# Two query groups whose weight tiles stream half of the tokens at a time: 256 + 128 columns in one, 128 columns throughout in the other

## The chip, the cores and the metric

The kernel runs on one NeuronCore of a Trainium2 chip. The metric is the device time of one execution in microseconds. The engines that matter here are TensorE (PE in the profile; its weight loads are listed apart as PEld), VectorE (DVE), ScalarE (ACT), and SyncE (SP), whose queue issues most transfers.

## The reference: what is computed

A decoder trunk of two layers over 256 tokens of width 2048, in float32: first a pooling mixer with a gated feed-forward part, then attention over one shared K and V with another gated feed-forward part. The change lies in the second layer, in one of three projections of the stream h (256 × 2048):

```python
k_shared = (h @ shared_w_k).reshape(B_, S, N_HEADS, HEAD_DIM)
v_shared = (h @ shared_w_v).reshape(B_, S, N_HEADS, HEAD_DIM)
...
q = (h @ w_q).reshape(B_, S, N_HEADS, HEAD_DIM)
```

Each weight matrix is 2048 × 2048, for 16 heads of 128. Behind them come three dilated causal windows, merged by their softmax denominators, and the output projection w_o.

## The kernel before

**Numbers.** A float32 product is made of three products of the format fp32r: each weight tile is split into a high part wh (ACT, line 82) and a low part wl (DVE, line 83), each activation likewise, and high × high, high × low and low × high are added up in PSUM. Low × low is left out.

**Units.** The whole program is a list of units. A unit is a weight tile of 512 rows by 512 columns (four blocks of 128 rows, k, by four blocks of 128 columns, m). `ahead` (line 110) issues the transfer of a unit's weights up to 5 units ahead on the SyncE queue, and the split up to 3 units ahead. `run_units` (line 125) takes one unit after the other: its matmuls, then whatever is due. `later(n, fn)` (line 119) puts work off by n units; what is due is counted in units.

**A unit's matmuls.** `mm_quad` (line 149) makes 16 pairs of (k, m). The activations of one quarter of the width lie in a tile `q` of shape 128 × 4 (k) × 2 (high, low) × 258, with 256 tokens used; they are the moving operand. A weight block of 128 × 128 is the stationary operand. In the mode "ab", which most units use, a pair is two matmuls: `h[:, k, c]` streams high and low side by side, 512 columns (line 164), into a PSUM bank of 512 columns, and `l[:, k, c]` streams the high part alone, 256 columns, onto the first half of that bank (line 165). The halves of the bank are added when it is read out. Modes "a" and "x" make three matmuls of 256 or 258 columns onto the first half (lines 167 to 169). Four banks, one for each m, collect four units (one group). In the last unit of a group the pairs go block by block (m outside, k inside), in the others k is outside. The first matmul onto a bank in a group clears it (`start`).

**The attention stage.** For hq = 0 to 3 (line 961) there are a k group, a q group and a v group of four units each. `group_tm` (the v groups) holds the activations stationary and streams weights, 512 columns each (lines 230 to 232). `qk_post` (line 856) reads a q or k group out of its banks: ACT copies the second half of a bank, DVE adds the first (lines 873, 874). Two and three units after a q group come its `scores` (line 883). `outputs` (line 948) of an hq runs four and seven units after its v group, so between the units of the next q group: matmuls at lines 956 and 957, then a split of the result on ACT and DVE (lines 958, 959) that gives the bank back. PSUM has 8 banks that all of these take in turn.

**Order.** Everything is emitted by hand in this order; each engine executes its own instructions in the order of emission and waits for others by semaphores.

Of the kernel before, what the change touches and what calls it, by code (L numbers as in the profile page):

```python
# [18 lines left out]
P = 128  # L19
# [13 lines left out]
def trunk(ctx: ExitStack, tc: tile.TileContext, x, pool_w_in, pool_w_grp, pool_scale, pool_w_out,  # L33
# [3 lines left out]
    V, A, PE = nc.vector, nc.scalar, nc.tensor  # L37
# [10 lines left out]
    def bank(nm):  # L48
        return psp.tile([P, 512], F32, name=nm, tag="ps")
# [69 lines left out]
    def later(n, fn):  # L119
        if n == 0:  # L120
            fn()
        else:
            pending.append([n, fn])
# [25 lines left out]
    def mm_quad(xq, ps, first, last, mode, mid, shifted):  # L149
        def go(h, l):  # L150
            nk, nb = h.shape[1], h.shape[2] // P
            order = [(k, m) for k in range(nk) for m in range(nb)]
            if last:
                order = [(k, m) for m in range(nb) for k in range(nk)]
            if first:
                for m in range(nb):
                    ps.append(bank("acc"))
            q = xq()
            n = XW if mode == "x" else T
            for i, (k, m) in enumerate(order):  # L160
                c = slice(m * P, (m + 1) * P)
                st, sp = first and k == 0, last and k == nk - 1
                if mode == "ab":
                    PE.matmul(ps[m], h[:, k, c], q[:, k, :, :T], start=st, stop=False)  # L164
                    PE.matmul(ps[m][:, :T], l[:, k, c], q[:, k, 0, :T], start=False, stop=sp and not shifted)  # L165
                else:
                    PE.matmul(ps[m][:, :n], h[:, k, c], q[:, k, 0, :n], start=st, stop=False)  # L167
                    PE.matmul(ps[m][:, :n], h[:, k, c], q[:, k, 1, :n], start=False, stop=False)  # L168
                    PE.matmul(ps[m][:, :n], l[:, k, c], q[:, k, 0, :n], start=False, stop=sp and not shifted)  # L169
                if sp and shifted:  # L170
                    PE.matmul(ps[m][:, :T], neg1, ST["cs"], start=False, stop=True)
                if mid is not None and i == 7:
                    mid()
        return go

    def group(w, r0s, c0, ncol, xqs, post, mode="ab", mids=(), shifted=False):
        ps = []
        for j, (r0, nr) in enumerate(r0s):
            last = j == len(r0s) - 1
            units.append((w[r0:r0 + nr, c0:c0 + ncol],  # L180
                          mm_quad(xqs[j], ps, j == 0, last, mode, mids[j] if j < len(mids) else None, shifted),
                          (lambda: post(ps)) if last else None))
# [98 lines left out]
    rows4 = [(512 * j, 512) for j in range(4)]  # L281
# [14 lines left out]
    xsrcs = [lambda j=j: XC[j] for j in range(4)]  # L296
# [146 lines left out]
    def norm_evac(ps, nb, tmp, dst):  # L443
        wgb = lnp.tile([P, 4, 2], F32, name="wgb", tag="wgb", bufs=2)
        for m in range(nb):
            A.copy(wgb[:, m, :], ps[m][:, T:XW])
        for m0 in range(0, nb, 2):
            ts = [(m, tmp()) for m in range(m0, min(nb, m0 + 2))]
            for m, t in ts:
                V.tensor_tensor(t, ps[m][:, :T], ST["rs"], OP.mult)  # L450
            for m, t in ts:
                V.scalar_tensor_tensor(t, ST["mr"], wgb[:, m, 0:1], t, op0=OP.mult, op1=OP.subtract)
                A.activation(dst(m), t, AF.Identity, scale=-1.0, bias=wgb[:, m, 1:2])
# [388 lines left out]
    def v_post(c):  # L842
        def post(t, ps):
            if t == 0:
                vts[c] = pools["attn"].tile([P, 2, 512], F32, name="vt", tag="vt")
                A.copy(vts[c][:, 0, :], ps)
            else:
                V.tensor_copy(vts[c][:, 1, :], ps)
                if c == 3:
                    later(1, lambda: transposes(c, (0, 1)))  # L850
                    later(2, lambda: transposes(c, (2, 3)))
                later(2 if c == 3 else 4, lambda: outputs(c, (0, 1)))
                later(3 if c == 3 else 7, lambda: outputs(c, (2, 3)))
        return post

    def qk_post(nm, hq):
        def post(ps):
            later(2 if hq == 0 and nm == "k" else 0, lambda: evac(ps))

        def evac(ps):  # L860
            ap = pools["attn"]
            o = ap.tile([P, 4, T], F32, name=nm, tag=nm)
            qk[nm] = o

            def tmp():
                return ap.tile([P, T], F32, name="qt", tag="t1", bufs=2)

            if hq == 0 and nm == "k":
                norm_evac(ps, 4, tmp, lambda m: o[:, m, :])
            else:  # L870
                for m in range(4):
                    t = tmp()
                    A.copy(t, ps[m][:, T:])
                    V.tensor_tensor(o[:, m, :], ps[m][:, :T], t, OP.add)
            if nm == "q":
                later(2, lambda: scores(hq, range(0, 2)))
                later(3, lambda: scores(hq, range(2, 4)))
                if hq < 3:
                    later(4, lambda: blocks(hq, (0, 1)))
                    later(7, lambda: blocks(hq, (2, 3)))  # L880
        return post

    def scores(hq, ms):
        ap = pools["attn"]
        for m in ms:
            ps = bank("s")
            q, k = qk["q"][:, m, :], qk["k"][:, m, :]
            PE.matmul(ps[:, 0:P], q[:, :P], k[:, :P], start=True, stop=True)
            PE.matmul(ps[:, P:3 * P], q[:, P:], k, start=True, stop=True)
            if m % 2 == 0:  # L890
                two = ap.tile([P, 2, 3, P], F32, name="p", tag="p", bufs=2)
            s = two[:, m % 2]
            sf, nf, cf = (t.rearrange("p a b -> p (a b)") for t in (s, negm, cnt))
            V.scalar_tensor_tensor(sf, ps[:, :3 * P], scale, nf, op0=OP.mult, op1=OP.add)
            mx = ap.tile([P, 6], F32, name="mx", tag="mx", bufs=4)
            parts = ((0, slice(0, P)), (1, slice(P, 3 * P)))
            for t, sl in parts:
                V.tensor_reduce(mx[:, t:t + 1], sf[:, sl], AX.X, OP.max)
            V.tensor_scalar(mx[:, 2:4], mx[:, 0:2], -1.0, None, op0=OP.mult)
            for t, sl in parts:  # L900
                A.activation(sf[:, sl], sf[:, sl], AF.Exp, bias=mx[:, 2 + t:3 + t])
            pr[hq, m] = (s, mx, two)
        for m in ms:
            s, mx, _ = pr[hq, m]
            sf, cf = (t.rearrange("p a b -> p (a b)") for t in (s, cnt))
            for t, sl in parts:
                V.scalar_tensor_tensor(sf[:, sl], sf[:, sl], 1.0, cf[:, sl], op0=OP.mult, op1=OP.mult,
                                       accum_out=mx[:, 4 + t:5 + t])
            V.reciprocal(mx[:, 0:2], mx[:, 4:6])
            for t, sl in parts:  # L910
                V.tensor_scalar(sf[:, sl], sf[:, sl], mx[:, t:t + 1], None, op0=OP.mult)
# [18 lines left out]
    def blocks(hq, ms):  # L930
        two = pr.pop((hq, ms[0]))[2]
        pr.pop((hq, ms[1]))
        b = hp.tile([P, 6 * P], F32, name="pb", tag="h")
        V.transpose(b, two.rearrange("p h s k -> p (h s k)"))

        t = turned(hq, ms)
        to = t.rearrange("p h s -> p (h s)").rearrange("p (k a j) -> p a k j", k=6, a=4)
        fr = b.rearrange("p (k b j) -> p b k j", k=6, b=4)

        def move(rows):  # L940
            for i in rows:
                for j in range(4):
                    nc.sync.dma_start(to[32 * j:32 * j + 32, i], fr[32 * i:32 * i + 32, j])

        later(1, lambda: move((0, 1)))
        later(2, lambda: move((2, 3)))
# [14 lines left out]
    for hq in range(4):  # L961
        x0 = hq == 0
        group(shared_w_k, rows4, 512 * hq, 512, psrcs if x0 else xsrcs, qk_post("k", hq), mode="x" if x0 else "ab")
        group(attn_w_q[0], rows4, 512 * hq, 512, xsrcs, qk_post("q", hq))
        group_tm(shared_w_v, rows4, 512 * hq, 512, xsrcs, v_post(hq))
    add_last(attn_w_o[0], rows4, [lambda j=j: oq[j] for j in range(4)], True, 1, 0, after=to_tokens)
    marks.append(len(units))
# [4 lines left out]
    with tc.tile_pool(name="start", bufs=1) as stp:  # L972
        for q in range(NQ):
            for t in range(2):
                XIN[q, t] = stp.tile([P, 512], F32, name=f"xin{q}{t}")
            halves = [slice(0, 256), slice(256, 512)] if q == 0 else [slice(0, 512)]
# [130 lines left out]
```

## Time and profile before

| | |
|---|---|
| runs: median (lowest to highest) | 2061.25 us (2060.78 to 2061.72), 2 runs |
| profiled execution: span from first to last instruction | 2060.0 us |
| TensorE busy | 2049.6 us, 99% |
| matmuls, weight loads | 11942 each |
| DVE, ACT busy | 73%, 50% |
| granted TensorE clock | 1.00 in the attention stage |
| q groups of hq = 1 and hq = 2 on TensorE | 22.87 and 22.84 us |

A row of a group shows line, engine, operation, tiles (written <- read), shapes and count, then busy time, the mean ns of one, and the idle time of the engine ahead of it with what ended it. A matmul's row reads 128*128 for the stationary block and 128x512 for the moving operand. Matmuls overlap in their rows, and a matmul's end is modelled; starts are the safer measure. The timeline gives start and duration in us from the span's start.

### The profile page before, as it was taken

How to read it: one execution, taken by the hardware profiler on the slowest of the kernel's cores; microseconds unless marked ns; L12 is line 12 of the kernel's file. 1: busy time of each engine (PE TensorE's matmuls, PEld its weight loads, DVE VectorE, ACT ScalarE, POOL GpSimd, SP SyncE). 2: the span in 40 equal slices, each digit the busy share in tenths (PEclk: the TensorE clock that was granted, in tenths of full speed). 3: DMA queues.
4: the chain of work that ended last, by engine and by line, in shares of the span. 5: the costliest groups of instructions: out<-in, count | busy, mean ns of one | idle time of the engine just before them, and what ended most of it. 6: DMA issues, size and time to landing. Idle time of an engine off the chain costs nothing.

```text
span 2060.0 us, 29055 instructions
## 1 busy us (share of the span) xinstructions
PE 2049.6 (99%) x11942; PEld 1799.5 (87%) x11942; DVE 1505.6 (73%) x1925; ACT 1032.9 (50%) x1139; POOL 36.5 (2%) x67
## 2 busy tenths in 40 slices
PE   9999999999999999999999999999999999999998
PEld 8999988888888888889888888998888888888887
DVE  6768877756756766779755667788886787676688
ACT  6445665345534535547544344575445544544552
POOL 2000000000000000000000000000010001000000
PEclk9999999999999999999999999999999999999999
DMA  8655565655555555555566555556686558556554
GB/s 269 212 189 189 173 197 172 203 184 185 184 196 191 171 198 180 182 183 172 191 193 200 174 169 179 179 180 186 190 253 219 189 164 265 184 164 222 166 184 164
DMA packets 236997, 393.71 MB, mean 191 GB/s; under 512 B 44878, under 2 KB 56292, under 8 KB 236608
## 3 DMA queue, kind: packets, MB, share of 16 engines
q1 hardware_dynamic: 231328, 385.52, 57.4%
q0 software_dynamic: 5104, 5.69, 1.7%
q8 instruction: 93, 1.52, 0.3%
q10 hardware_dynamic: 432, 0.66, 0.1%
q14 instruction: 40, 0.33, 0.0%
HBM read 380.01 MB, written 2.10 MB: 185 GB/s over the span
## 4 chain that ended last, share of the span: by engine, by line
PE 91%; DVE 4%; DMA 2%; ACT 1%; issue 1%; SPq 0%; POOL 0%; DVEq 0%; ACTq 0%; POOLq 0%
PE acc L164 47%; PE acc L165 24%; PE t L231 3%; PE t L230 3%; PE t L232 3%; PE acc L168 3%; PE acc L169 3%; PE acc L167 3%; DVE wl L83 1%; DMA raw<-in_ffn_w_up_dram 1%; ACT wh L82 1%; DMA raw<-in_ffn_w_down_dram 1%; DMA ht<-u 0%; ACT wh L95 0%; DVE wl L96 0%
## 5 line engine op out<-in xcount | busy, mean ns | idle before, releaser
L164 PE MATMUL acc<-xc,wh 128*128 128x512 f32 x3264 | 1149.5, 396 | 0.0
L83 DVE TENSOR_TENSOR wl<-raw,wh 128x2048 fp32r<-128x2048 f32 (+2 forms) x365 | 795.5, 2184 | 405.2 <-ACT wh L82 395.5
L82 ACT CAST wh<-raw 128x2048 fp32r<-128x2048 f32 (+2 forms) x365 | 664.2, 1825 | 535.5 <-PE acc L164 346.7
L165 PE MATMUL acc<-xc,wl 128*128 128x256 f32 x3264 | 915.9, 281 | 0.0
L164 PEld LDWEIGHTS acc<-xc,wh 128*128 128x128 f32 x3264 | 615.7, 189 | 145.7 <-DVE o L959 0.6
L165 PEld LDWEIGHTS acc<-xc,wl 128*128 128x128 f32 x3264 | 615.5, 189 | 0.2
L164 PE MATMUL acc<-g,wh 128*128 128x512 f32 x644 | 226.8, 396 | 0.0
L165 PE MATMUL acc<-g,wl 128*128 128x256 f32 x644 | 180.6, 280 | 0.0
L164 PEld LDWEIGHTS acc<-g,wh 128*128 128x128 f32 x644 | 121.5, 189 | 28.4
L592 DVE SCALAR_TENSOR_TENSOR c<-u,cv,c 128x256 f32<-128x256 f32 x344 | 141.6, 478 | 0.5
L165 PEld LDWEIGHTS acc<-g,wl 128*128 128x128 f32 x644 | 121.7, 189 | 0.0
L579 ACT COPY ut<-acc 128x256 f32<-128x256 f32 x164 | 58.8, 371 | 95.7 <-PE acc L165 95.4
L231 PE MATMUL t<-wl,g 128*128 128x512 f32 (+1 forms) x267 | 102.8, 385 | 0.3 <-DVE wl L83 0.3
L230 PE MATMUL t<-wh,g 128*128 128x512 f32 (+1 forms) x267 | 103.0, 386 | 0.0
L232 PE MATMUL t<-wh,g 128*128 128x512 f32 (+1 forms) x267 | 102.6, 384 | 0.0
L588 ACT ACTIVATE c<-u,cv 128x256 f32<-128x256 f32 x172 | 89.6, 596 | 3.1 <-DVE u L580 3.1
L580 DVE TENSOR_TENSOR u<-acc,ut 128x256 f32<-128x256 f32 x164 | 60.9, 416 | 30.7 <-ACT ut L579 30.7
L164 PE MATMUL acc<-o,wh 128*128 128x512 f32 x192 | 67.9, 396 | 0.0
L164 PE MATMUL acc<-mixed,wh 128*128 128x512 f32 x192 | 67.5, 395 | 0.0
L278 ACT CAST g<-c 128x1024 fp32r<-128x1024 f32 (+1 forms) x22 | 22.6, 1029 | 84.4 <-DVE c L658 84.4
L231 PEld LDWEIGHTS t<-wl,g 128*128 128x128 f32 x267 | 50.2, 188 | 11.1 <-DVE wl L83 1.1
L232 PEld LDWEIGHTS t<-wh,g 128*128 128x128 f32 x267 | 50.1, 188 | 11.0
(265 smaller groups left out, 2358.7 us busy)
## 6 DMA issues: line engine op xcount, KB each, us to landing
raw<-in_ffn_w_up_dram SPq DMA_DIRECT2D x160, 1024.0 KB, 5.1
raw<-in_ffn_w_down_dram SPq DMA_DIRECT2D x80, 1024.0 KB, 5.1
raw<-in_pool_w_out_dram SPq DMA_DIRECT2D x16, 1024.0 KB, 5.0
raw<-in_shared_w_k_dram SPq DMA_DIRECT2D x16, 1024.0 KB, 5.1
raw<-in_attn_w_q_dram SPq DMA_DIRECT2D x16, 1024.0 KB, 5.2
raw<-in_shared_w_v_dram SPq DMA_DIRECT2D x16, 1024.0 KB, 5.8
raw<-in_attn_w_o_dram SPq DMA_DIRECT2D x16, 1024.0 KB, 5.0
raw<-in_pool_w_in_dram SPq DMA_DIRECT2D x12, 1024.0 KB, 5.7
```

Of the source, the lines that this page charges most:

```text
L82: A.copy(wh[i][:, s], r[:, s])
L83: V.tensor_tensor(wl[i][:, s], r[:, s], wh[i][:, s].bitcast(F32), OP.subtract)
L164: PE.matmul(ps[m], h[:, k, c], q[:, k, :, :T], start=st, stop=False)
L165: PE.matmul(ps[m][:, :T], l[:, k, c], q[:, k, 0, :T], start=False, stop=sp and not shifted)
L167: PE.matmul(ps[m][:, :n], h[:, k, c], q[:, k, 0, :n], start=st, stop=False)
L168: PE.matmul(ps[m][:, :n], h[:, k, c], q[:, k, 1, :n], start=False, stop=False)
L169: PE.matmul(ps[m][:, :n], l[:, k, c], q[:, k, 0, :n], start=False, stop=sp and not shifted)
L230: PE.matmul(to, xh, h[:, k, c], start=j == 0 and k == 0, stop=False)
L231: PE.matmul(to, xh, l[:, k, c], start=False, stop=False)
L232: PE.matmul(to, xl, h[:, k, c], start=False, stop=j == len(r0s) - 1 and k == nk - 1)
L588: A.activation(c[:, m, :], u[:, m, 2:], AF.Identity, scale=cv[:, 2, j:j + 1], bias=cv[:, 3, j:j + 1])
L592: V.scalar_tensor_tensor(c[:, m, :], u[:, m, i:i + T], cv[:, i, j:j + 1], c[:, m, :], op0=OP.mult, op1=OP.add)
```

## The change

`mm_quad` gets two more modes. Both take the 256 tokens in two halves of 128 (`t`). In "halves", a weight block `h` streams 128 tokens of the high part and the same 128 of the low part in one matmul of 256 columns (two pieces of 128 on either side), then `l` streams the 128 tokens of the high part. In "thirds" the matmul with `h` is cut in two as well, so that all are of 128 columns. Products, sums and the places in the bank are the same. The q group of hq = 1 uses "halves", that of hq = 2 "thirds", four units each; the q groups of hq = 0 and 3 stay with "ab". No other engine's instructions change.

```diff
@@ mm_quad
-                if mode == "ab":
+                if mode in ("halves", "thirds"):
+                    two = ps[m].rearrange("p (s t) -> p s t", s=2)
+                    for t in range(2):
+                        ts = slice(t * P, t * P + P)
+                        if mode == "halves":
+                            PE.matmul(two[:, :, ts], h[:, k, c], q[:, k, :, ts], start=st and t == 0, stop=False)
+                        else:
+                            PE.matmul(two[:, 0, ts], h[:, k, c], q[:, k, 0, ts], start=st and t == 0, stop=False)
+                            PE.matmul(two[:, 1, ts], h[:, k, c], q[:, k, 1, ts], start=False, stop=False)
+                        PE.matmul(ps[m][:, ts], l[:, k, c], q[:, k, 0, ts], start=False, stop=sp and t == 1)
+                elif mode == "ab":
                     PE.matmul(ps[m], h[:, k, c], q[:, k, :, :T], start=st, stop=False)
                     PE.matmul(ps[m][:, :T], l[:, k, c], q[:, k, 0, :T], start=False, stop=sp and not shifted)
@@ the attention stage
-        group(attn_w_q[0], rows4, 512 * hq, 512, xsrcs, qk_post("q", hq))
+        group(attn_w_q[0], rows4, 512 * hq, 512, xsrcs, qk_post("q", hq),
+              mode={1: "halves", 2: "thirds"}.get(hq, "ab"))
```

## The prediction

> **What bounds the kernel now.** I read the engine totals first, then the chain that ended last, then the stretches of the two groups that change, and last single instructions in them.
>
> ```profile
> span 2060.0 us, 29055 instructions
> ...
> PE 2049.6 (99%) x11942; PEld 1799.5 (87%) x11942; DVE 1505.6 (73%) x1925; ACT 1032.9 (50%) x1139; POOL 36.5 (2%) x67
> ...
> PE 91%; DVE 4%; DMA 2%; ACT 1%; issue 1%; SPq 0%; POOL 0%; DVEq 0%; ACTq 0%; POOLq 0%
> ...
> L164 PE MATMUL acc<-xc,wh 128*128 128x512 f32 x3264 | 1149.5, 396 | 0.0
> ...
> L165 PE MATMUL acc<-xc,wl 128*128 128x256 f32 x3264 | 915.9, 281 | 0.0
> L164 PEld LDWEIGHTS acc<-xc,wh 128*128 128x128 f32 x3264 | 615.7, 189 | 145.7 <-DVE o L959 0.6
> ```
>
> TensorE is busy for 99% of the span and holds 91% of the chain, so time added to its stream shows in the end almost one for one. There are as many weight loads (PEld) as matmuls, 11942 of each: every matmul has a load of its own. The durations in the groups (396, 281, 189 ns) can't be added up, because neighbours overlap. What counts is the step from one start to the next. In the timeline the columns are start and duration in us:
>
> ```profile
> 1118.06 0.39 PE L164 MATMUL acc<-xc,wh 128*128 128x512 f32 x1
> 1118.29 0.28 PE L165 MATMUL acc<-xc,wl 128*128 128x256 f32 x1
> 1118.41 0.40 PE L164 MATMUL acc<-xc,wh 128*128 128x512 f32 x1
> ...
> 1118.06 0.19 PEld L165 LDWEIGHTS acc<-xc,wl 128*128 128x128 f32 x1
> 1118.29 0.19 PEld L164 LDWEIGHTS acc<-xc,wh 128*128 128x128 f32 x1
> 1118.41 0.19 PEld L165 LDWEIGHTS acc<-xc,wl 128*128 128x128 f32 x1
> ```
>
> 512 columns take 0.23 us, 256 columns 0.12 us: time goes with columns, about 0.46 ns each. The load for the next matmul starts together with the current one (1118.06, 1118.29, 1118.41), so it has the length of the current matmul to hide in. Here that is at least 0.12 us.
>
> The stretches, by windows (start:end, length, busy time and count of each engine, granted clock, DMA):
>
> ```profile
> 1015.68:1038.21 22.53, 22.53 (x129) 19.65 (x128) 13.91 (x9) 8.09 (x6) 0.00 (x0) 1.00 0.68 203
> ...
> 1039.44:1056.55 17.11, 17.11 (x100) 14.82 (x98) 9.14 (x9) 7.26 (x8) 0.00 (x0) 1.00 0.67 200
> 1057.77:1063.53 5.76, 5.76 (x36) 5.03 (x35) 3.95 (x6) 3.19 (x5) 0.00 (x0) 1.00 0.35 137
> 1112.21:1129.30 17.09, 17.09 (x99) 14.81 (x98) 9.14 (x9) 7.25 (x8) 0.00 (x0) 1.00 0.69 200
> 1130.53:1136.28 5.75, 5.75 (x36) 5.02 (x34) 3.95 (x6) 3.19 (x5) 0.00 (x0) 1.00 0.35 135
> ```
>
> The first row is the k group ahead of the second q group, 128 matmuls of the pair form without interruption: 22.53 us for 64 pairs is **352 ns a pair** (234 and 118). The other four rows are the q groups of hq = 1 and hq = 2, three units and then one, with attention matmuls between: 22.87 and 22.84 us, 45.71 us in all. In each TensorE is busy throughout while DVE and ACT are below 70% of the stretch, and the clock is 1.00. So TensorE alone sets the pace there.
>
> **The change part by part.** Each group has 4 units of 16 pairs, 64 pairs. The columns stay the same, 768 a pair. What grows is the number of instructions.
>
> Halves (hq = 1): a pair becomes 4 matmuls, 256 + 128 + 256 + 128 columns: 128 more matmuls and 128 more loads in the group. Thirds (hq = 2): 6 matmuls of 128 columns: 256 more of each. If only columns counted, a 128-column matmul would take half of the 118 ns step, 59 ns, and a pair 354 ns in either form.
>
> But the load for the next matmul must then fit into 59 ns. Call x the step after a 128-column matmul. The after-change time of a pair is 2 × (118 + x) in halves and 6x in thirds; against 352, 64 pairs of each:
>
> added = 64 × (236 + 2x − 352 + 6x − 352) ns = **0.512x − 29.95 us** (x in ns).
>
> No stream of 128-column matmuls of this number format is in the trace before, so x is bounded. It needs the time that a load takes when nothing covers it. That is seen where TensorE had run dry and a matmul had to wait for its own load:
>
> ```profile
> 1481.17 0.19 PEld L231 LDWEIGHTS t<-wl,g 128*128 128x128 f32 x1 [0.49 <-DVE wl L83]
> 1481.18 0.49 PE L231 MATMUL t<-wl,g 128*128 128x512 f32 x1
> 1481.28 0.19 PEld L232 LDWEIGHTS t<-wh,g 128*128 128x128 f32 x1
> 1481.51 0.39 PE L232 MATMUL t<-wh,g 128*128 128x512 f32 x1
> ...
> 1506.54 0.39 PE L220 MATMUL t<-wl,g 128*128 128x256 f32 x1 [0.21 <-DVE wl L96]
> 1506.77 0.28 PE L221 MATMUL t<-wh,g 128*128 128x256 f32 x1
> 1506.88 0.28 PE L219 MATMUL t<-wh,g 128*128 128x256 f32 x1
> ```
>
> The L231 matmul is 0.10 us longer than the 0.39 of the next, and the step after it is 0.33 us instead of 0.23. The L220 matmul has a step of 0.23 instead of 0.11 to 0.12. The next load (1481.28) starts 0.11 us after the one before it, although nothing else occupied the array. All three say that a load holds the weight path for about 0.11 us and that the next one starts only when the matmul that uses the former has begun. The 0.19 us of a load's row is then latency beside occupancy: in the stream, loads start 0.12 us apart and overlap in their rows.
>
> So behind a 128-column matmul the load is the longer part, and I take **x = 110 ns**. Above, x is bounded by 118 ns, the step of 256 columns, within which every load fits today. Below by 59 ns, the columns alone. A pair is then 456 ns in halves and 660 ns in thirds: 64 × 104 = 6.7 us and 64 × 308 = 19.7 us, 26.4 us together. The ends give 0.3 us (59) and 30.5 us (118).
>
> I take the row nearest in kind: the exposed loads are of the same weight tiles, type and width as in the q groups. Nothing hides the added 26.4 us: in the five windows above TensorE has no idle time that it could fill, and DVE and ACT, which do, aren't awaited.
>
> One stall goes. On the first unit of each of the two groups a matmul waits for a PSUM bank that the attention output before it (L959) gives back:
>
> ```profile
> 1113.22 0.28 PE L165 MATMUL acc<-xc,wl 128*128 128x256 f32 x1
> ...
> 1113.38 0.19 PEld L164 LDWEIGHTS acc<-xc,wh 128*128 128x128 f32 x1 [0.19 <-DVE o L959]
> 1113.38 0.50 PE L164 MATMUL acc<-xc,wh 128*128 128x512 f32 x1
> ...
> 1113.72 0.28 PE L165 MATMUL acc<-xc,wl 128*128 128x256 f32 x1
> ```
>
> From 1113.22 to 1113.72 it is 0.50 us instead of 0.35: 0.15 us lost to the wait and to the load behind it, which nothing covers. It is the fourth pair, the opening of the fourth bank; three longer pairs put it 0.3 us (halves) or 0.9 us (thirds) later, past that wait. Both groups have it: −0.3 us. Next in line then is only TensorE's own stream.
>
> A gain beyond that is excluded as far as the rows go: 512 columns take 234 ns and two times 256 take 236, so shorter pieces are not quicker per column.
>
> No DMA, no DVE or ACT work and no issue of either is added or moved. Units, their order, splits, transfers and the waiting list, which counts units and not time, are as before. A longer unit gives the splits and transfers of later units more time. Evacuation starts, as before, behind the last matmul of each bank; the last unit takes the blocks one after the other in both forms. Instruction fetch gains 768 entries on TensorE, two per 110 ns in the densest stretch against two per 118 ns in stretches of 256 columns that run without gaps.
>
> Sum: 26.4 − 0.3 = **26.1 us**. The profiled execution would go from a span of 2060.0 to 2086.1 us. The median of the runs, 2061.25, lies 1.25 us above the span, so 2061.25 + 26.1 = 2087.4 us.
>
> **The Trainium skill against this.** The page "TensorE: Matmul & The Clock Gate", section "Back-to-back issue gap", gives about 81 ns per matmul for a sustained stream of load and matmul pairs at 128 columns, and about 131 ns at 512. By 81 ns the sum would be 0.512 × 81 − 29.95 = 11.5 us and the time, with the stalls gone, 2072.5 us, an estimate from that page. The trace doesn't agree with its other figure, since 512 columns take 234 ns here. The same page's section on "Weight-path perf modes" says that the fast weight load doesn't apply to FP32 weights; no run here shows that.
>
> **The rivals.**
>
> *The loads hide wholly* (x = 59): the other side, not slower. The place is the step after every 128-column matmul, the price 0.3 us, and the stalls stay since the pairs are hardly longer, so 2061.6 us. It decides for as long as a load takes under 59 ns. For it: the loads start early and overlap in their rows. Against it: the exposed loads of 0.11 us.
>
> *Short loads*: a load takes less than 110 ns when they come thick. These transposes load 128 columns each, four in a row:
>
> ```profile
> 39.21 0.14 PEld L1027 LDWEIGHTS vT<-ident,vrow 80*128 80x128 f32 x1
> ...
> 39.33 0.36 PEld L1039 LDWEIGHTS cT<-ident,crow 86*128 86x128 f32 x4
> ```
>
> A single load is 0.14 us and four end after 0.36, so they start (0.36 − 0.14) / 3 = 0.073 us apart. With x = 73 the sum is 7.4 us, the time 2068.6 us (the stalls at most 0.3 less). Against it: these loads have rows of 0.14 us instead of 0.19, so they are of another kind. The skill's 81 ns, above, would fall into this case.
>
> *The second load of the same weights is left out* in thirds, where two matmuls in a row use one wh block; the change would then not do quite what it says. A pair would be 2 × (59 + 110 + 110) = 558 ns, the group 13.2 us longer, the whole 13.2 + 6.7 − 0.3 = 19.6 us: 2080.9 us. Against it are forms that do this already, L167 and L168, with a load for each:
>
> ```profile
> L167 PEld LDWEIGHTS acc<-o,wh 128*128 128x128 f32 x64 | 12.1, 190 | 0.0
> ...
> L168 PEld LDWEIGHTS acc<-o,wh 128*128 128x128 f32 x64 | 12.1, 188 | 0.0
> ```
>
> *The load's whole row counts* (x = 189): nothing overlaps once the matmul is shorter than the load. 0.512 × 189 − 29.95 = 66.8 us, less the stalls 66.5: 2127.8 us. Against it: loads 0.11 to 0.12 us apart with rows of 0.19. To pass 2% (41.2 us) x would have to be over 139 ns, above the bound of 118.
>
> **How the numbers follow.** Forecast (x from about 105 to 118, 2085 to 2092): 0.80. Short loads 0.07, left-out loads 0.04, hidden wholly 0.04, whole row 0.05. The forecast alone just reaches 0.8; I take the range on to the left-out loads below and to slightly over the bound of 118 above: 2079 to 2093. A change of 2% is about what a measurement of this kernel can tell from no change; the forecast is 1.3%, slower but within it. Slower by over 2% is the whole-row case, 0.05; faster by over 2% has no case, 0.01 for what I don't see; within 2% 0.94.
>
> **What the profile of the changed kernel would show.** TensorE with 384 more matmuls and as many loads (12326). The group of hq = 1 in 29.4 us instead of 22.87, that of hq = 2 in 42.4 instead of 22.84. In the timeline steps of 0.12 and 0.11 us by turns in halves and 0.11 throughout in thirds, each load starting with a matmul. No wait at the fourth pair. Everything else in its place, later by the sum. Wrong would be steps near 0.06 or 0.07 (loads hidden or short), 0.19 (whole row), fewer loads than matmuls, or a k, v or output stretch that changes its length.

## The result

The changed kernel takes 2089.88 us (median of 2 runs, 2089.3 to 2090.45) against 2061.25 us: ratio **1.0135**, 95% interval 1.0117 to 1.0153. It is slower by 28.6 us; the forecast was 26.1 us and 2087.4 us. TensorE's busy time grows by the same 28.6 us.

The page after, totals and chain:

```profile
span 2087.5 us, 29823 instructions
...
PE 2078.2 (100%) x12326; PEld 1834.8 (88%) x12326; DVE 1506.1 (72%) x1925; ACT 1033.4 (50%) x1139; POOL 36.5 (2%) x67
...
PE 92%; DVE 4%; DMA 2%; ACT 1%; issue 1%; SPq 0%; POOL 0%; DVEq 0%; ACTq 0%; POOLq 0%
```

384 matmuls and 384 loads more; DVE, ACT and POOL have the same number of instructions and, to 0.5 us, the same busy time. The two q groups after the change, by windows, in the same order as in the prediction (hq = 1 in the first two rows, hq = 2 in the last two):

```profile
1040.79:1063.16 22.37, 22.37 (x195) 22.37 (x194) 9.15 (x9) 7.24 (x8) 0.00 (x0) 1.00 0.60 175
1064.44:1071.89 7.45, 7.45 (x67) 7.45 (x66) 4.23 (x6) 3.19 (x5) 0.00 (x0) 1.00 0.20 52
1120.62:1152.82 32.20, 32.20 (x292) 32.20 (x290) 9.15 (x9) 7.23 (x9) 0.00 (x0) 1.00 0.45 141
1154.09:1164.84 10.75, 10.75 (x99) 10.75 (x98) 4.33 (x6) 3.29 (x6) 0.00 (x0) 1.00 0.27 99
```

The group in halves takes 29.82 us instead of 22.87, the one in thirds 42.95 instead of 22.84: 72.77 us in place of 45.71, 27.1 us more. The PEld busy time (behind that of PE) now equals the length of the stretch; before the change it was 14.82 of 17.11. That alone doesn't show that the loads bind: a load's row has 0.19 us, so rows that start 0.12 us apart or less overlap and leave no gap, whatever sets the step. The run with wh cut, below, has 17.33 of 17.38 at hardly any cost.

The span grew by 27.5 us. The other 0.4 us comes from outside the groups. Ahead of them the matmuls of after already lie 1.35 us later than those of before: about 0.4 us of it by a longer wait for the input (the longest 1.8 us against 1.4), the rest where the clock of TensorE fell for some microseconds in this execution. About 1 us comes back at the very end, where the wait ahead of the last matmuls is shorter; small shifts make up the rest. The row of the start (7.30 to 11.00 us), first of after, then of before:

```profile
7.30:11.00 3.70, 3.63 (x20) 3.41 (x21) 2.22 (x4) 2.44 (x4) 0.00 (x0) 0.68 0.94 323
```

```profile
7.30:11.00 3.70, 3.48 (x28) 3.07 (x26) 2.73 (x4) 2.45 (x4) 0.00 (x0) 1.00 0.99 317
```

The granted clock is 0.68 in one and 1.00 in the other, before any changed instruction. The waits of TensorE at the end, before and then after:

```profile
PE gb L823 <- DVE dg L821: 1.8, 1, 1.8
```

```profile
PE gb L833 <- DVE dg L831: 0.8, 1, 0.8
```

Single instructions show where the load bites. First halves, then thirds, in the timeline of after:

```profile
1049.85 0.23 PE L172 MATMUL acc<-xc,wl 128*128 128x128 f32 x1
1049.85 0.19 PEld L168 LDWEIGHTS acc<-xc,wh 128*128 128x128 f32 x1
1049.91 0.33 PE L168 MATMUL acc<-xc,wh 128*128 128x256 f32 x1
1049.96 0.19 PEld L172 LDWEIGHTS acc<-xc,wl 128*128 128x128 f32 x1
1050.08 0.23 PE L172 MATMUL acc<-xc,wl 128*128 128x128 f32 x1
1050.09 0.19 PEld L168 LDWEIGHTS acc<-xc,wh 128*128 128x128 f32 x1
...
1155.02 0.28 PE L172 MATMUL acc<-xc,wl 128*128 128x128 f32 x1
1155.07 0.19 PEld L170 LDWEIGHTS acc<-xc,wh 128*128 128x128 f32 x1
1155.13 0.27 PE L170 MATMUL acc<-xc,wh 128*128 128x128 f32 x1
1155.18 0.19 PEld L171 LDWEIGHTS acc<-xc,wh 128*128 128x128 f32 x1
1155.24 0.28 PE L171 MATMUL acc<-xc,wh 128*128 128x128 f32 x1
1155.29 0.19 PEld L172 LDWEIGHTS acc<-xc,wl 128*128 128x128 f32 x1
```

In thirds everything steps by 0.11 us. In halves read the **loads**: 1049.85, 1049.96, 1050.09, so 0.11 and 0.12 to 0.13 by turns. The matmuls' own starts mislead: they step by 0.06 (1049.85 to 1049.91) and 0.17. The rows fit this reading: a matmul's row begins when the one before it has finished streaming, and where its weights are still on their way the wait is inside the row. So the 256-column matmul has 0.33 us instead of the 0.28 of before, and a 128-column one has 0.27 to 0.28 in thirds, where its load is exposed, against 0.23 in halves, where 256 columns cover its load.

### The profile page after: what moved, and what is told of

The parts are those of the page before. It is cut to its first block, busy times and chain, and to the rows that moved or that the text cites. A ratio compares the mean times of both kernels' runs of the same rounds, so it can differ in the third digit from the quotient of the medians.

```text
span 2087.5 us, 29823 instructions
## 1 busy us (share of the span) xinstructions
PE 2078.2 (100%) x12326; PEld 1834.8 (88%) x12326; DVE 1506.1 (72%) x1925; ACT 1033.4 (50%) x1139; POOL 36.5 (2%) x67
## 4 chain that ended last, share of the span: by engine, by line
PE 92%; DVE 4%; DMA 2%; ACT 1%; issue 1%; SPq 0%; POOL 0%; DVEq 0%; ACTq 0%; POOLq 0%
PE acc L174 45%; PE acc L175 23%; PE t L241 3%; PE t L240 3%; PE t L242 3%; PE acc L178 3%; PE acc L179 3%; PE acc L177 3%; PE acc L172 1%; PE acc L168 1%; DVE wl L83 1%; DMA raw<-in_ffn_w_up_dram 1%; PE acc L171 1%; PE acc L170 1%; ACT wh L82 1%
## 5 line engine op out<-in xcount | busy, mean ns | idle before, releaser
L174 PE MATMUL acc<-xc,wh 128*128 128x512 f32 x3136 | 1103.6, 395 | 0.0
L175 PE MATMUL acc<-xc,wl 128*128 128x256 f32 x3136 | 879.9, 281 | 0.0
L174 PEld LDWEIGHTS acc<-xc,wh 128*128 128x128 f32 x3136 | 591.6, 189 | 139.8 <-DVE o L969 0.2
L175 PEld LDWEIGHTS acc<-xc,wl 128*128 128x128 f32 x3136 | 591.4, 189 | 0.2
L172 PE MATMUL acc<-xc,wl 128*128 128x128 f32 x256 | 63.8, 249 | 0.0
```

The costliest lines, as they stand in the source:

```text
L172: PE.matmul(ps[m][:, ts], l[:, k, c], q[:, k, 0, ts], start=False, stop=sp and t == 1)
```

## The experiments

Theory A: the step from one matmul to the next is the larger of two times, that of its columns and that of one weight load, about 111 ns. Rival B: every further matmul, or the cut into pieces of 128 tokens, has a cost of its own. Rival C: repeating the load of a block costs because it is a repeat, or is left out. Times stand against runs of the kernel before on the same chip, 2062.02 us (first four) and 2061.86 us (last four).

**Cut wh or cut wl.** Both have three matmuls, three loads and 768 columns a pair in both groups, and compute everything. One keeps every matmul at 256 columns, the other has two of 128.

```diff
 cut_high
+                    for t in range(2):
+                        ts = slice(t * P, t * P + P)
+                        PE.matmul(two[:, :, ts], h[:, k, c], q[:, k, :, ts], start=st and t == 0, stop=False)
+                    PE.matmul(ps[m][:, :T], l[:, k, c], q[:, k, 0, :T], start=False, stop=sp)
 cut_low
+                    PE.matmul(ps[m], h[:, k, c], q[:, k, :, :T], start=st, stop=False)
+                    for t in range(2):
+                        ts = slice(t * P, t * P + P)
+                        PE.matmul(ps[m][:, ts], l[:, k, c], q[:, k, 0, ts], start=False, stop=sp and t == 1)
```

> Both groups (hq 1 and 2) cut only the wh matmul by tokens: 256 + 256 columns, then wl with 256 uncut; 3 matmuls and 3 loads a pair, the full computation. Theory A (the step after a matmul is the larger of its columns, 0.46 ns each, and one load of about 111 ns): no matmul is shorter than a load, a pair takes 3 x 118 = 354 ns, 128 pairs add 0.3 us: about 2061.5 us, the same as the kernel before. Rival B (each further matmul, or cutting into pieces of 128 tokens, costs its own 56 ns, which is what the changed group of hq 1 shows for each of its two further matmuls a pair): 128 x 56 ns = 7.2 us more, about 2068.5 us.

> Both groups cut only the wl matmul: wh with 512 columns, wl with 128 + 128; as many matmuls, loads and columns as where wh is cut, the full computation. Theory A: 234 + 2 x 112 = 458 ns a pair against 352, 128 pairs add 13.6 us: about 2075 us, 13 us more than where wh is cut. Rival B: again 56 ns for the one further matmul, 7.2 us, about 2068.5 us, equal to where wh is cut.

With wh cut: 2062.21 us, ratio 1.0003 (0.9994 to 1.0012), no change. With wl cut: 2075.23 us, ratio 1.0066 (1.005 to 1.0083), 13.0 us more than with wh cut, where theory A had 13 and B nothing. The first three units of the second group, wh cut, then wl cut:

```profile
1112.91:1130.29 17.38, 17.38 (x148) 17.33 (x147) 9.14 (x9) 7.26 (x9) 0.00 (x0) 1.00 0.68 199
```

```profile
1120.13:1142.05 21.92, 21.92 (x147) 19.79 (x146) 9.15 (x9) 7.25 (x8) 0.00 (x0) 1.00 0.59 176
```

Before it was 17.09. Same number of matmuls, and 0.3 against 4.8 us more. So the further matmul and the strided pieces of 128 tokens cost little by themselves: 0.3 us over 48 pairs is 6 ns for each further matmul, where B had 56. The price is on matmuls shorter than a load. B falls.

**Widths.** Six matmuls a pair with other numbers of columns, in all q groups.

```diff
-              mode={1: "halves", 2: "thirds"}.get(hq, "ab"))
+              mode={0: 64, 1: 160, 2: 208, 3: 240}.get(hq, "ab"))
...
+                    for t in range(2):
+                        PE.matmul(ps[m][:, :mode], h[:, k, c], q[:, k, 0, :mode], start=False, stop=False)
+                        PE.matmul(ps[m][:, T:T + mode], h[:, k, c], q[:, k, 1, :mode], start=False, stop=False)
+                        PE.matmul(ps[m][:, :mode], l[:, k, c], q[:, k, 0, :mode], start=False, stop=sp and t == 1)
```

> The form with 6 matmuls and 6 loads a pair in all four q groups, each on the first 64 (hq 0), 160 (hq 1), 208 (hq 2) or 240 (hq 3) tokens, twice; the first unit of each group stays as before, 48 pairs are of the new form. Streams other columns than the reference asks for, so q is not the reference's. Theory A: the step is 111 to 112 ns at 64, 160, 208 and 240 columns alike (240 columns by themselves are 0.46 x 240 = 110), and the four q groups take about the same time, 5.6 + 288 x 0.1115 = 37.7 us each. Rival B (52 ns on top of the columns for every short matmul): 82, 126, 148 and 162 ns, groups of 29, 42, 48 and 52 us.

Stretches of 160, 208 and 240 columns and then, in the last row, of 64:

```profile
1088.30:1109.60 21.30, 21.30 (x193) 21.30 (x192) 4.96 (x3) 3.81 (x2) 0.00 (x0) 1.00 0.46 154
1176.30:1197.60 21.30, 21.30 (x193) 21.30 (x192) 4.95 (x3) 3.80 (x2) 0.00 (x0) 1.00 0.54 168
1264.30:1285.80 21.50, 21.50 (x193) 21.50 (x192) 4.95 (x3) 3.81 (x2) 0.00 (x0) 1.00 0.51 165
985.00:1006.00 21.00, 21.00 (x100) 21.00 (x100) 5.08 (x9) 3.71 (x5) 0.00 (x0) 0.50 0.29 98
```

192 loads in 21.30 us are 0.111 us each, at 160 columns as at 208, and 0.112 at 240: a **floor**. Columns don't matter until they fill it by themselves, at about 240. At 64 columns the expectation missed: 0.21 us a step. The clock in that row is 0.50 instead of 1.00, and the load takes twice as long with it (one run, 2148.12 us). More on that below.

**Smaller blocks.** Matmuls of 128 columns with 64 or 32 of the block's columns, or 64 of its rows, in 44 of 64 pairs.

```diff
-              mode={1: "halves", 2: "thirds"}.get(hq, "ab"))
+              mode={1: (64, 128), 2: (32, 128), 3: (128, 64)}.get(hq, "ab"))
...
+                    nm, nr = mode
+                    c = slice(m * P, m * P + nm)
+                    for t in range(2):
+                        ts = slice(t * P, t * P + P)
+                        PE.matmul(two[:nm, 0, ts], h[:nr, k, c], q[:nr, k, 0, ts], start=False, stop=False)
+                        PE.matmul(two[:nm, 1, ts], h[:nr, k, c], q[:nr, k, 1, ts], start=False, stop=False)
+                        PE.matmul(ps[m][:nm, ts], l[:nr, k, c], q[:nr, k, 0, ts], start=False, stop=sp and t == 1)
```

> The form of 6 matmuls of 128 tokens a pair with smaller weight blocks, in 44 of the 64 pairs of a group: 64 of the 128 output columns (hq 1), 32 of them (hq 2), 64 of the 128 rows (hq 3). Leaves out the rest of the products, so q is not the reference's. Theory A with a load that takes as long as it has columns: 55 and 28 ns for 64 and 32 columns, shorter than 128 streamed columns, so the step is 59 to 62 ns and both groups take about 23 us as before the change; with half of the rows the load stays, step 111 ns and a group of 36 us. Theory A with a load of fixed length, and rival B: 111 ns in all three, 36 us each.

64 columns of the block, then 32, then half of the rows after some time; below them, in the timeline, the first steps with half of the rows:

```profile
1046.90:1058.50 11.60, 11.60 (x194) 11.60 (x192) 5.01 (x3) 3.82 (x2) 0.00 (x0) 1.00 0.75 223
1120.50:1131.90 11.40, 11.40 (x193) 11.40 (x192) 4.97 (x3) 3.81 (x2) 0.00 (x0) 1.00 0.69 206
1211.00:1232.00 21.00, 21.00 (x101) 21.00 (x100) 2.29 (x1) 1.90 (x1) 0.00 (x0) 0.50 0.14 50
```

```profile
1193.91 0.19 PEld L170 LDWEIGHTS acc<-xc,wh 64*128 64x128 f32 x1
...
1194.02 0.19 PEld L171 LDWEIGHTS acc<-xc,wl 64*128 64x128 f32 x1
...
1194.14 0.19 PEld L169 LDWEIGHTS acc<-xc,wh 64*128 64x128 f32 x1
```

With 64 block columns a step is 11.60 / 192 = 0.060 us, with 32 it is 0.059: as many streamed columns, as many loads, and the whole excess of 0.05 us is gone. A block with fewer columns also writes fewer rows of its PSUM bank, but writing can't be what the 128-column matmul waits for, since 160 and 208 columns write more and step no slower. So it waits for the load, and the load is shorter when the block has fewer columns: at most 0.060 us with half of them. How much shorter isn't shown, since the streamed columns take that long themselves. With half of the rows the first loads still step by 0.11 us, as expected; then the clock falls to 0.50 and the steps double, which was not expected (one run, 2107.19 us).

**One at a time.**

```diff
-              mode={1: "halves", 2: "thirds"}.get(hq, "ab"))
+              mode={1: "halves"}.get(hq, "ab"))     # halves_alone
+              mode={2: "thirds"}.get(hq, "ab"))     # thirds_alone
```

> The change in hq 1 alone, hq 2 as before. Theory A (step = the larger of the columns and one load): steps of 118 to 122 and 110 to 112 ns, 64 pairs longer by 108 to 113 ns, a stall of 0.15 us gone: about 6.9 us more than the kernel before. If the two groups' costs depended on each other (a shared stall, the clock), the two single changes would not add up to the 28 us of both.

> The change in hq 2 alone. Theory A: six steps of 112 ns a pair against 352 ns, 64 pairs: 20.5 us, a stall of 0.15 us gone: about 20.3 us more than the kernel before; with hq 1 alone it adds up to 27 us.

Halves alone: 2069.35 us, 7.5 us more, ratio 1.0035 (1.0022 to 1.0048). Thirds alone: 2082.56 us, 20.7 us more, ratio 1.0099 (1.0082 to 1.0116). Together 28.2 us, and both at once measured 28.6; each interval leaves some 3 us to either side. The traces are sharper: three units and one take 22.37 and 7.46 us in halves alone, 32.19 and 10.75 us in thirds alone, the same to 0.01 us as with both. The groups don't influence each other.

**Same block side by side.**

```diff
-              mode={1: "halves", 2: "thirds"}.get(hq, "ab"))
+              mode={1: "cut", 2: "cut"}.get(hq, "ab"))
...
+                    tss = [slice(0, P), slice(P, 2 * P)]
+                    for t, ts in enumerate(tss):
+                        PE.matmul(two[:, :, ts], h[:, k, c], q[:, k, :, ts], start=st and t == 0, stop=False)
+                    for t, ts in enumerate(tss):
+                        PE.matmul(ps[m][:, ts], l[:, k, c], q[:, k, 0, ts], start=False, stop=sp and t == 1)
```

> Both groups take the halves with the two matmuls of one weight block side by side: wh 256, wh 256, wl 128, wl 128; the full computation. Theory A (each matmul needs a load of its own, and each load starts only when the matmul before it does): 118 + 118 + 112 + 112 = 460 ns a pair, 128 pairs 13.8 us, stalls of 0.3 us gone: 13.5 us more than the kernel before, as if the two were apart. Rival C (the second load of the same block is left out or costs nothing): the step after the first wl matmul is 60 ns, a pair 408 ns, 7 us more.

2075.94 us, 14.1 us more, ratio 1.0066 (1.0051 to 1.0081). Theory A had 13.5, rival C 7. In the trace the first three units take 22.24 us, 463 ns a pair, against 466 with the two apart: a block that was loaded just before is loaded again, at full price and no more. C falls; the 12326 loads for 12326 matmuls in the page of after say the same.

**More widths**, for the clock that fell at 64 columns:

```diff
+              mode={0: 112, 1: 96, 2: 80}.get(hq, "ab"))
```

> The form of 6 matmuls a pair on the first 112 (hq 0), 96 (hq 1) and 80 (hq 2) tokens, twice, in 48 of 64 pairs of the q groups, hq 3 as before; streams other columns than the reference asks for, so q is not the reference's. Theory A: 111 to 112 ns a step wherever the granted clock is 1.00. The clock fell to 0.50 at 64 columns a step and held at 128; if it follows the share of time in which columns stream (0.24 at 64, 0.48 at 128), it holds at 112 and falls at 80, and at 96 it is open; where it falls, a load and so the step take 213 ns.

112 columns, then 96 and 80 over their whole stretches:

```profile
975.90:1007.70 31.80, 31.80 (x288) 31.80 (x287) 17.82 (x19) 13.34 (x20) 0.00 (x0) 1.00 0.48 165
1062.50:1119.70 57.20, 57.20 (x296) 56.84 (x295) 9.42 (x9) 7.47 (x8) 0.00 (x0) 0.56 0.24 81
1176.50:1231.80 55.30, 55.30 (x296) 54.94 (x295) 9.39 (x9) 7.47 (x8) 0.00 (x0) 0.58 0.27 89
```

At 112 columns the clock holds and the step is 0.11 us. At 96 and at 80 it is 0.50 most of the time (0.56 and 0.58 in the mean). In the stretch with 96 it comes back to 1.00 from 1103.6 to 1106.9 us, and there the loads step by 0.11 us again: the step follows the clock. The edge lies between 96 and 112 columns behind loads of 0.11 us (one run).

## Why the prediction was right

- **The bound.** TensorE sets the end; the 27.1 us that its two groups grew by came out as 27.5 us of span. Nothing absorbed it, and the k groups kept their 22.53 us.
- **x, the step behind 128 columns.** Taken as 110 ns from three signs at two exposed loads; measured 112 ns in thirds (32.20 us for 48 pairs is 671 ns a pair, predicted 660). Over the group the forecast lacked 64 × 11 ns = 0.7 us by it.
- **Halves.** 22.37 us for 48 pairs is 466 ns a pair, predicted 456: 0.6 us over the group. The load behind the 256-column matmul starts 0.12 to 0.13 us after the one before it, where the prediction had 118 ns. Why a 256-column matmul takes some 4 ns longer here than in a stream of its kind stays open. With wl cut, the uncut 512-column matmul behind short ones is likewise 2 to 3 ns longer (loads 0.236 us apart instead of 0.234), so the cut into pieces need not be the whole reason.
- **The stall at the fourth pair.** It went. The loads' rows in the groups of the page of after, the pairs left as they were first, then those of halves and thirds:

```profile
L174 PEld LDWEIGHTS acc<-xc,wh 128*128 128x128 f32 x3136 | 591.6, 189 | 139.8 <-DVE o L969 0.2
```

```profile
L170 PEld LDWEIGHTS acc<-xc,wh 128*128 128x128 f32 x128 | 24.6, 192 | 0.0
L168 PEld LDWEIGHTS acc<-xc,wh 128*128 128x128 f32 x128 | 24.3, 190 | 0.0
```

  The idle time that the attention output ended was 0.6 us before and is 0.2 now, and the changed pairs have none.
- **The size.** The sum was 26.1 us; the groups took 27.1 us more, the span 27.5, the median of the runs 28.6. The first miss of 1.0 us is two errors that partly cancel, which is luck. The two steps above make 1.3 us too little. Against it, the prediction let 0.3 us go, but the two groups before lay 0.65 us above two times the 22.53 us of the k group. The missing 0.35 us is a wait it had no term for: behind attention matmuls, four times in the two groups, the load of the first block is exposed, and the step is 0.31 to 0.32 us instead of 0.23. In before:

```profile
1039.44 0.48 PE L164 MATMUL acc<-xc,wh 128*128 128x512 f32 x1
1039.76 0.28 PE L165 MATMUL acc<-xc,wl 128*128 128x256 f32 x1
```

  In the changed groups a load sets the step at every other matmul (halves) or at every one (thirds), so most of this is no longer an extra. The miss between groups and span is the start and the end of the execution, which the change doesn't touch; the last 1.1 us is within the spread of two runs on either side (0.9 and 1.2 us). The remark that a change of 2% is about what can be told from none was too cautious: the intervals here and for halves alone (1.0022 to 1.0048) both exclude 1.
- **The rivals.** *Hidden wholly* and *short loads* would have shown steps of 0.06 or 0.07; the loads step by 0.11. The reason given against short loads held: the transposes' loads (rows of 0.14 us) are not those of these weights. The Trainium skill's 81 ns per matmul ("TensorE: Matmul & The Clock Gate", "Back-to-back issue gap") doesn't hold for this number format: 112 ns here. The same page of the Trainium skill says in "LDWEIGHTS (loading the stationary operand)" that a load's time goes with the block's columns and not with its rows. The run with smaller blocks agrees: 0.060 us or less with half of the columns, 0.11 with half of the rows at the full clock. *Left-out loads* fell with the blocks side by side. *Whole row*: rows of 0.19 us overlap at steps of 0.11.
- **One marker failed.** "Steps of 0.12 and 0.11 us by turns in halves" is true of the loads. The matmuls' starts show 0.17 and 0.06. Nor does each load start with a matmul: the load at 1049.96 lies between the matmuls at 1049.91 and 1050.08, and in thirds every load starts 0.05 us behind a matmul. A reader who had gone by matmuls alone would have taken the 0.06 for hidden loads; the 0.33 us rows and the loads' starts say otherwise.

## What to carry to other kernels

A stream of matmuls with changing weights has a floor of one weight load a matmul: 111 ns for 128 block columns in this format at the full clock, as long as about 240 streamed columns. Cut down to that width and it costs next to nothing (three times 256 instead of 512 + 256 was the same to 0.1%); cut below it and every matmul pays the difference. Where loads bind, read the starts of the loads, not those of the matmuls, and hold their step against the time of the columns alone. Load rows that fill the stretch are no sign: with wh cut they filled 17.33 of 17.38 us for 0.3 us more, with wl cut only 19.79 of 21.92 us for 4.8 us more.

## What was not expected of the hardware

The clock of TensorE can fall in a stretch in which it never rests. With matmuls of 64, 80 or 96 columns behind loads of 0.11 us, or 128 columns with half of the rows, the granted clock went to 0.50 within the stretch and the load itself took twice as long, 0.21 us. With 112 columns and more, and with blocks of 64 or 32 columns at 0.060 us a step, it stayed at 1.00. Estimates from 0.46 ns a column and these steps: at 64, 80 and 96 columns the array is streaming for 26, 33 and 40% of the time, at 112 and 128 for 46 and 53% (the expectation had 0.24 at 64 and 0.48 at 128). With half of the rows it is again 53%, but through half of the array's rows, as much as 26% through all of them. The page "TensorE: Matmul & The Clock Gate" of the Trainium skill, section "What's actually happening", has the gate follow how busy TensorE has been recently. The runs fit that if busy means streamed columns times rows, and not instructions in progress, since the rows of TensorE fill each of these stretches without a gap. The block's own columns don't seem to count, as 32 of 128 held the clock. This is a reading of one run of each form, not shown beyond them. The changed kernel's thirds, 128 columns at a step of 0.11, are not far above that edge.
